# Eight gate modulation tiles of the second layer, computed among the first layer's heads instead of at the layer boundary

## The chip, the cores and the metric

The kernel runs on one core of a Trainium2 chip. The metric is the device time of one execution in microseconds (us); the kernel before was run three times. One execution was recorded by the hardware profiler, and its trace is what all rows below are read from. The engines are named as in the trace: PE is the matrix engine (PEld its weight loads), DVE the vector engine, ACT the scalar engine, POOL is GpSimd, SP issues transfers.

## The reference

One inference step of a two-layer decoder. T = 1088 token columns (1024 of a prompt, 8 x 8 of samples), D = 1024, 8 heads of 128. Each layer modulates a normalised input with shift and scale that come from a conditioning vector, mixes, projects out and adds the result with a gate from the same vector:

```python
def ada_modulate(x, c, norm_g, ada_w, ada_b):
    mod = jnp.einsum('bd,de->be', jax.nn.silu(c), ada_w) + ada_b
    shift, scale, gate = jnp.split(mod[:, None, :], 3, axis=-1)
    h = rms_norm(x, norm_g) * (1 + scale) + shift
    return h, gate

# layer 0, mixer_a: proj = h @ w_in; causal conv and silu on q, k, v; per head a gated
#   delta rule in chunks of 64 (a triangular solve per chunk, then a scan over the chunks);
#   o = rms_norm(o) * silu(z); y = o @ w_out
# layer 1, mixer_b: proj = h @ w_in; three groups of dilated window attention
#   (128, 1), (512, 4), (2048, 16), for samples over a cache of keys and values;
#   mixed by their log sums; y = (o * silu(z)) @ w_out
# x = x + gate * y after each layer; a last rms_norm
```

The `mod` row of one layer has 3072 columns, that is 24 tiles of 128: 8 of shift, 8 of scale, 8 of gate. A layer's gate is needed only when its output projection is added; its shift and scale are needed when its input is modulated.

## The kernel before, in words

All activations stand transposed: 128 features on the partitions, 1088 tokens along them, in three column chunks of 384, 384 and 320. `project` (L117 to L137) is one projection to 128 features: for each chunk, 8 k-tiles with three products each (hi by hi, hi by lo, lo by hi of operands split in two), 72 matmuls at L129, into one of two PSUM banks named pp; the third chunk takes the bank of the first once that has been copied out. Its weights come as one 512 KB transfer from SP's queue into `wraw` (L104, two buffers) and are split by ACT into `whi` (L110) and by DVE into `wlo` (L111), two buffers each.

One **modulation tile** (`ada_tile`, L145) is a 512 KB load of 128 columns of `ada_w`, 8 matmuls at L153 (the trace records each twice, so x16 is one tile), an ACT copy (`adr`, L155), one matmul at L160 (recorded twice too) and a DVE addition of the bias at L170, which writes `SH`, `SC` or `GT`. A generator (`ada_tiles`) hands out the tiles in a list, one for each credit that `ada.pump` gives.

Layer 0 runs over heads, in this program order: `stage_k(0)`, `stage_qv(0)`, `stage_k(1)`, `stage_inverse(0)`, and then for each head h: the scan of h, the q and v projections of h + 1, the k projection of h + 2 and the inverse of h + 1. So the projections come as k0, q0, v0, k1, q1, v1, k2 and so on; v0 is the v projection of head 0. Between them PE does small matmuls of the heads: kk products (L658), a short chain of powers for the inverse (`Us` and `su`, L680 to L693), transposes to natural order (L603), qk products (L740), the triangular inverse (L780 to L819), sample states (L845 to L913) and the scan (L932 to L946). The chain of the inverse needs the gates of all heads (`gall`, L522 to L526, and a round trip through memory, `gcscr` to `DT`, L646).

`conv_tile` (L549) is a projection of a head followed by the causal convolution; it ends with `ada.pump(1)`, except for k0. So 23 of the 24 listed tiles (layer 0's gate, layer 1's shift and scale) are handed out in the heads through `wraw`, and one more by `ada.pump(100)` after them (L1005).

At the layer boundary layer 1's input is modulated (`modulate`, L193 to L214): a column pass of 768 first, under the out projection, and then a last pass of 320 columns, tile by tile (j = 0 to 7). Each j takes some DVE operations (L72, the helper of scalar_tensor_tensor, and L201 to L210); ACT casts the result to `hh` and DVE or POOL subtracts to get `hl`. In this last loop (L1084 to L1086) each j is followed by `ada.pump(1)`, which hands out one of layer 1's eight gate tiles; their loads have a pool of their own, `aw`, of two buffers (`ada_load`, L139, transfer L142).

After it come layer 1's set-up (masks `mt` and `mdec` at L1133, three masks `Z` set to zero at L1140) and its first projection, of V in group 2 and head 0, whose result is copied out of PSUM at L1178 on DVE, 128x384 for the first two chunks. K's copies stand at L1176 on ACT.

A scheduler sets the order of the instructions on each engine from the program and its own estimates; an engine then works its list off in that order, each instruction waiting for what it needs. So an edit in one place can move instructions of many others.

Of the kernel before, what the change touches and what calls it, by code (L numbers as in the profile page):

```python
# [8 lines left out]
F32 = mybir.dt.float32  # L9
# [5 lines left out]
P = 128  # L15
D = 1024
KD = D // P
# [25 lines left out]
def kernel(ctx, tc, I, O):  # L43
# [58 lines left out]
    def wraw(src, n=P):  # L102
        t = wp.tile([P, KD, P], F32, name="wraw", bufs=2)
        SY.dma_start(out=t[:, :, :n], in_=src.rearrange("(k p) n -> p k n", p=P))  # L104
        return t
# [30 lines left out]
                        next(woven[0], None)  # L136
            cb(ci, acc)  # L137

    def ada_load(layer, ct, pool, ahead):  # L139
        src = I["ada_w"][layer, :, ct * P:(ct + 1) * P]  # L140
        t = pool.tile([P, KD, P], F32, name="aw", bufs=ahead)
        SY.dma_start(out=t, in_=src.rearrange("(k p) n -> p k n", p=P))  # L142
        return t

    def ada_tile(layer, ct, w):  # L145
        ada_fold(layer, ct, ada_rows(w))

# [92 lines left out]
            if not self.todo:  # L240
                self.credit = 0.0

    def ada_tiles(pool, todo):
        def load(i):
            layer, ct = todo[i]
            return ada_load(layer, ct, pool, 2) if pool else wraw(I["ada_w"][layer, :, ct * P:(ct + 1) * P])
        w = load(0) if pool else None
        for n, (layer, ct) in enumerate(todo):
            nxt = load(n + 1) if pool and n + 1 < len(todo) else None
            ada_tile(layer, ct, w if pool else load(n))  # L250
            w = nxt
            yield

    ada = Units()
    ada.todo.append(ada_tiles(None, [(0, c) for c in range(16, 24)] + [(1, i + o) for i in range(8) for o in (8, 0)]))


    W0 = I["a_w_in"][0]
# [45 lines left out]
    with tc.tile_pool(name="n0", bufs=1) as n0:  # L304
        aw = []
# [243 lines left out]
    def conv_tile(t, dst):  # L549
        w = wsplit(wraw(W0[:, t * P:(t + 1) * P]), G if 8 <= t < 16 else V)  # L550
        prev = [None]

        def cb(ci, acc):
            cn = CHUNKS[ci][1]
            xin = sb.tile([P, 387], F32, name="xin", bufs=2)
            if ci == 0:
                G.memset(xin[:, 0:3], 0.0)
            else:
                G.tensor_copy(out=xin[:, 0:3], in_=prev[0][:, 384:387])
            prev[0] = xin  # L560
            if ci < 2:
                A.copy(out=xin[:, 3:3 + cn], in_=acc[:, :cn])
                W = cn
            else:
                A.copy(out=xin[:, 3:259], in_=acc[:, :256])
                xs = xin[:, 259:347].rearrange("p (b x) -> p b x", x=11)
                G.tensor_copy(out=xs[:, :, 0:3], in_=scT[:, t, :].rearrange("p (b i) -> p b i", i=3))
                A.copy(out=xs[:, :, 3:11], in_=sview(acc[:, 256:320]))
                W = 344
                cst = sb.tile([P, 27], F32, name="cst", bufs=2)  # L570
                G.tensor_copy(out=cst[:, 0:3], in_=xin[:, 256:259])
                G.tensor_copy(out=cst[:, 3:27].rearrange("p (b i) -> p b i", i=3), in_=xs[:, :, 8:11])
                ct = acc[:27, 320:320 + P]
                PE.transpose(ct, cst, ident)
                cso = sb.tile([27, P], F32, name="cso", bufs=2)
                V.tensor_copy(out=cso, in_=ct)
                SY.dma_start(out=conv_p[:, t * P:(t + 1) * P], in_=cso[0:3, :])
                SY.dma_start(out=conv_s[:, t * P:(t + 1) * P], in_=cso[3:27, :])
            ca = sb.tile([P, 387], F32, name="ca", bufs=2)
            A.activation(out=ca[:, :W], in_=xin[:, 0:W], func=AF.Copy, scale=cwT[:, 0, t:t + 1])  # L580
            for i in range(1, 4):
                stt(ca[:, :W], xin[:, i:i + W], cwT[:, i, t:t + 1], ca[:, :W], ALU.mult, ALU.add)
            th = xin
            A.activation(out=th[:, :W], in_=ca[:, :W], func=AF.Tanh)
            c0 = CHUNKS[ci][0]
            if ci < 2:
                stt(dst[:, c0:c0 + cn], th[:, :cn], 1.0, ca[:, :cn], ALU.add, ALU.mult)
            else:
                stt(dst[:, c0:NP], th[:, :256], 1.0, ca[:, :256], ALU.add, ALU.mult)
                v1 = th[:, 259:347].rearrange("p (b x) -> p b x", x=11)[:, :, 0:8]  # L590
                v2 = ca[:, 259:347].rearrange("p (b x) -> p b x", x=11)[:, :, 0:8]
                stt(sview(dst[:, NP:]), v1, 1.0, v2, ALU.add, ALU.mult)
        project(w, hh, hl, cb)
        if t != 8:
            ada.pump(1)

    def banks_natural(src):
        out = []
# [409 lines left out]
    first.close()  # L1008
    set_banks(ctx, ps=3, lv=2, sc=1)

    aps = ExitStack()
    ap = aps.enter_context(tc.tile_pool(name="ap", bufs=1, reuse_waits="tile"))
    zp = ExitStack()
    zpool = zp.enter_context(tc.tile_pool(name="zp", bufs=1, reuse_waits="tile"))
    oh[7], ol[7] = (zpool.tile([P, T], F32R, name=n) for n in ("oh7", "ol7"))
# [47 lines left out]
    x1scr = [dr.tile([P, T], F32, name=f"x1scr{j}") for j in range(KD)]  # L1063
    x1 = [Columns("hh", F32) for _ in range(KD)]
    hh, hl = new_h()
    ada.todo.append(ada_tiles(ap, [(1, c) for c in range(16, 24)]))
    with tc.tile_pool(name="mid", bufs=1, reuse_waits="tile") as mp:
        def norm(qs, b0, b1):
            rn = col_stats(qs, b0, b1)
            rB = mp.tile([P, WIDE], F32, name="rB")  # L1070
            row_bcast(rB, rn, b0, b1)
            return rB

        def post(j):
            SY.dma_start(out=x1scr[j][:, :WIDE], in_=x1[j][:, :WIDE])

        def post2(j):
            SY.dma_start(out=x1scr[j][:, WIDE:], in_=x1[j][:, WIDE:])
            modulate(1, j, x1[j], rB, mp, hh, hl, 0, WIDE, True)
        qs = out_project(mp, 0, I["a_w_out"][0], xscr, x1, oh, ol, post, PASSES[0])  # L1080
        rB = norm(qs, 0, WIDE // P)
        qs = out_project(mp, 0, I["a_w_out"][0], xscr, x1, oh, ol, post2, PASSES[1])
        rB = norm(qs, WIDE // P, NC + 1)
        for j in range(KD):  # L1084
            modulate(1, j, x1[j], rB, mp, hh, hl, WIDE, T, j % 2 and j < KD - 1)
            ada.pump(1)  # L1086
    zp.close()
    aps.close()
    l0.close()


# [45 lines left out]
    Z = [sd.tile([P, ZW * n], F32, name=f"Z{g}").rearrange("p (b x) -> p b x", b=2 * NB)  # L1137
         for g, n in enumerate((1, 4, 8))]
    for t in Z:
        V.memset(t, 0.0)  # L1140
    odS = sd.tile([P, 512], F32, name="odS")
    G.memset(odS, 0.0)
    comb = sd.tile([P, 4, NL], F32, name="comb")
# [18 lines left out]
    def proj_tile(g, part, h, dst, dsts):  # L1162
        col = ((part * NG + g) * NH + h) * P
        w = wsplit(wraw(W1_[:, col:col + P]))

        def cb(ci, acc):
            c0, cn = CHUNKS[ci]
            n = cn if ci < 2 else cn - NS
            todo = [(perm(dst, g, c0, n), pin(acc, g, n))]
            if ci == 2:  # L1170
                todo.append((dsts[:, h % 2, :], acc[:, n:cn]))
            for o, i in todo:
                if part == 0:
                    A.activation(out=o, in_=i, func=AF.Copy, scale=-SCALE)
                elif part == 1:
                    A.copy(out=o, in_=i)  # L1176
                else:
                    V.tensor_copy(out=o, in_=i)  # L1178
        project(w, hh, hl, cb)

    def to_natural(src, nat, blocks, eng):
# [420 lines left out]
```

## Time and profile before

| | us |
|---|---|
| median of 3 runs | 2420.28 |
| lowest, highest | 2412.72, 2430.17 |
| the profiled execution's own time | 2412.29 |
| its span in the trace | 2410.6 |
| mean granted clock of PE | 0.962 of full speed |

The span runs from the first to the last instruction; 1.7 us of the execution lie around it. The profiled execution lies 8.0 us under the median, at the fast end of the runs. In a row, "x" counts instructions; a bracket in a timeline is the engine's idle time before the instruction and what ended it; the granted clock is a share of 2.4 GHz.

### The profile page before, as it was taken

How to read it: one execution, taken by the hardware profiler on the slowest of the kernel's cores; microseconds unless marked ns; L12 is line 12 of the kernel's file. 1: busy time of each engine (PE TensorE's matmuls, PEld its weight loads, DVE VectorE, ACT ScalarE, POOL GpSimd, SP SyncE). 2: the span in 40 equal slices, each digit the busy share in tenths (PEclk: the TensorE clock that was granted, in tenths of full speed). 3: DMA queues.
4: the chain of work that ended last, by engine and by line, in shares of the span. 5: the costliest groups of instructions: out<-in, count | busy, mean ns of one | idle time of the engine just before them, and what ended most of it. 6: DMA issues, size and time to landing. Idle time of an engine off the chain costs nothing.

```text
span 2410.6 us, 43253 instructions
## 1 busy us (share of the span) xinstructions
PE 2250.9 (93%) x16647; PEld 2116.5 (88%) x16647; DVE 1375.5 (57%) x3414; ACT 937.6 (39%) x2477; POOL 257.6 (11%) x418
## 2 busy tenths in 40 slices
PE   7899889999999998999998999899998999999998
PEld 5788778788888997999898999899998999989897
DVE  6678767867784437336733555434655336375334
ACT  5445445455443325233233332333323333234234
POOL 2213322333221103100000000000000000000000
PEclk9889989899999999999999999999999999999998
DMA  9223222223333445448822697535966349786634
GB/s 314 69 74 86 76 68 76 79 69 91 79 87 89 120 149 162 131 146 265 272 66 71 218 301 246 167 100 183 332 222 211 98 143 337 198 267 180 203 101 149
DMA packets 482255, 379.42 MB, mean 157 GB/s; under 512 B 46206, under 2 KB 457071, under 8 KB 482048
## 3 DMA queue, kind: packets, MB, share of 16 engines
q1 hardware_dynamic: 482048, 376.65, 51.6%
q8 instruction: 131, 2.15, 0.4%
q14 instruction: 76, 0.62, 0.1%
HBM read 322.31 MB, written 54.27 MB: 156 GB/s over the span
## 4 chain that ended last, share of the span: by engine, by line
PE 65%; DMA 11%; DVE 11%; issue 7%; ACT 3%; POOL 1%; SPq 1%; POOLq 0%; ACTq 0%; DVEq 0%
PE pp L129 47%; PE ps L1238 2%; PE ps L1220 2%; DMA DT<-gcscr 2%; PE sc L1438 2%; DMA wraw<-in_a_w_in_dram 2%; DVE vtmp L713 2%; DMA qb<-qscr 1%; PE ps L1184 1%; DVE pr L1389 1%; PE ps L1229 1%; DVE ca L72 1%; DMA oscr<-stgc 1%; PE ps L153 1%; DMA out_y_p_dram<-yn 1%
## 5 line engine op out<-in xcount | busy, mean ns | idle before, releaser
L129 PE MATMUL pp<-hh,whi 128*128 128x384 f32 (+1 forms) x2688 | 914.3, 341 | 14.5 <-DVE vT L1178 5.8
L129 PE MATMUL pp<-hl,whi 128*128 128x384 f32 (+1 forms) x2688 | 904.0, 336 | 1.3 <-POOL hl L214 1.3
L129 PE MATMUL pp<-hh,wlo 128*128 128x384 f32 (+1 forms) x2688 | 900.8, 335 | 2.0 <-DVE wlo L111 2.0
L129 PEld LDWEIGHTS pp<-hh,whi 128*128 128x128 f32 x2688 | 512.5, 191 | 29.8 <-DVE vT L1178 8.5
L129 PEld LDWEIGHTS pp<-hl,whi 128*128 128x128 f32 x2688 | 512.8, 191 | 6.6 <-issue 1.9
L129 PEld LDWEIGHTS pp<-hh,wlo 128*128 128x128 f32 x2688 | 511.3, 190 | 7.7 <-issue 2.9
L111 DVE TENSOR_TENSOR wlo<-wraw,whi 128x1024 fp32r<-128x1024 f32 x136 | 171.2, 1259 | 131.3 <-ACT whi L110 130.5
L110 ACT CAST whi<-wraw 128x1024 fp32r<-128x1024 f32 x144 | 150.7, 1046 | 230.0 <-PE pp L129 148.2
L1225 ACT ACTIVATE sm<-sm,stg 128x128 f32<-128x128 f32 (+1 forms) x192 | 86.6, 451 | 340.4 <-DVE stg L1223 299.8
L1389 DVE TENSOR_TENSOR pr<-kc,qb 128x1024 f32<-128x1024 f32 x128 | 154.9, 1218 | 85.2 <-DMA qb<-qscr 55.7
L1379 DVE TENSOR_REDUCE ST<-pr 128x8 f32<-128x1024 f32 x128 | 153.7, 1213 | 1.1
L438 POOL TENSOR_TENSOR ol<-zo,oh 128x384 fp32r<-128x384 f32 x9 | 9.1, 1013 | 1311.4 <-ACT oh L437 1291.2
L72 DVE SCALAR_TENSOR_TENSOR ca<-xin,cwT,ca 128x384 f32<-128x384 f32 (+1 forms) x216 | 129.0, 601 | 7.1 <-ACT ca L580 5.9
L1223 DVE CUSTOM_DVE_ANT_0 sm<-ps,mA 128x256 f32<-128x256 f32 (+1 forms) x128 | 48.3, 377 | 139.4 <-PE ps L1220 138.2
L1238 PE MATMUL ps<-vnat,pT 128*128 128x128 f32 x560 | 97.1, 281 | 8.1 <-DVE pT L1234 6.4
L713 DVE TENSOR_TENSOR vtmp<-Vi,Mi 128x2 f32<-128x2 f32 (+30 forms) x248 | 99.0, 399 | 4.2 <-POOL so L88 0.7
L1238 PEld LDWEIGHTS ps<-vnat,pT 128*128 128x128 f32 x560 | 86.1, 190 | 14.3 <-issue 4.8
L1220 PE MATMUL ps<-kT,qT 128*128 128x128 f32 (+1 forms) x384 | 93.5, 325 | 1.2 <-DVE stg L1223 1.2
L1232 ACT COPY pT<-ps 128x256 f32<-128x256 f32 (+1 forms) x96 | 32.4, 337 | 119.3 <-PE ps L1229 118.4
L72 DVE SCALAR_TENSOR_TENSOR hh<-pp,GT,xr 128x384 f32<-128x384 f32 (+1 forms) x48 | 27.4, 571 | 82.4 <-PE pp L129 78.7
L129 PE MATMUL pp<-oh,whi 128*128 128x384 f32 (+1 forms) x216 | 71.7, 333 | 2.7 <-DVE zt L72 2.7
L129 PE MATMUL pp<-oh,wlo 128*128 128x384 f32 (+1 forms) x216 | 71.9, 334 | 1.5 <-DVE wlo L111 1.5
(449 smaller groups left out, 3556.1 us busy)
## 6 DMA issues: line engine op xcount, KB each, us to landing
qb<-qscr SPq DMA_DIRECT2D x128, 512.0 KB
kc<-in_cache_kv_w_dram SPq DMA_DIRECT2D x104, 512.0 KB
vc<-in_cache_kv_w_dram SPq DMA_DIRECT2D x104, 512.0 KB
wraw<-in_b_w_in_dram SPq DMA_DIRECT2D x80, 512.0 KB
wraw<-in_a_w_in_dram SPq DMA_DIRECT2D x32, 512.0 KB
wraw<-in_ada_w_dram SPq DMA_DIRECT2D x24, 512.0 KB
stgc<-gscr SPq DMA_DIRECT2D x32, 260.0 KB
aw<-in_ada_w_dram SPq DMA_DIRECT2D x8, 1024.0 KB
```

Of the source, the lines that this page charges most:

```text
L72: return (eng or V).scalar_tensor_tensor(out=out, in0=in0, scalar=scalar, in1=in1, op0=op0, op1=op1)
L110: A.copy(out=hi, in_=raw)
L111: (eng or V).tensor_tensor(out=lo, in0=raw, in1=hi.bitcast(F32), op=ALU.subtract)
L129: mm = PE.matmul(acc[:, :cn], lhsT=a[:, k, :], rhs=b[k][:, c0:c0 + cn], start=(n == 0), stop=(n == 3 * KD - 1))
L713: V.tensor_tensor(out=tv, in0=Vi[:, :na, :w], in1=Mi[:, :w, c].unsqueeze(1).broadcast_to([P, na, w]), op=ALU.mult)
L1220: PE.matmul(sv, lhsT=qT[:, b * P:(b + 1) * P], rhs=kT[:, k0:k0 + w], start=True, stop=True)
L1223: V.tensor_tensor_reduce(out=sm[:, :w], in0=sv, in1=mk, scale=1.0, scalar=3e38, op0=ALU.add, op1=ALU.min, accum_out=stg[:, b, 128:129])
L1225: A.activation(out=sm[:, :w], in_=sm[:, :w], func=AF.Exp, scale=-1.0, bias=stg[:, b, 128:129], accum_out=stg[:, b, 129:130])
L1238: PE.matmul(ob[:, (b % 4) * P:(b % 4 + 1) * P], lhsT=pT[:, i * P:(i + 1) * P], rhs=vnat[:, k0 // P + i, :], start=(i == 0), stop=(i == w / ...
L1379: V.tensor_reduce(out=sv[:, n:n + 4, :], in_=pr.rearrange("p (n a e) -> p n a e", a=2, e=P), op=ALU.add, axis=AX.X)
L1389: V.tensor_tensor(out=out, in0=k, in1=q, op=ALU.mult)
L1438: mm = PE.matmul(od[32 * j:32 * j + 8, f * P:(f + 1) * P], lhsT=Z[g][:, a * NB + 2 * j + c, 8 * k:8 * k + 8], rhs=vc[:, j, a * P:(a + 1) * P],
```

## The change

It does three things. The eight gate tiles of layer 1 go into the same list as the other 24 and are loaded through `wraw`; `ada_load` and the pool `aw` go. The pump in `conv_tile` gives three credits instead of one after q0, v0 and k1 (t = 0, 16 and 9), so that the 23 pumps hand out 29 of 32 tiles and `ada.pump(100)` the last three. The three masks `Z` are set to zero by POOL instead of DVE. The first V projection, and that alone, is copied out of PSUM by ACT instead of DVE.

```diff
-    def ada_load(layer, ct, pool, ahead):
-        src = I["ada_w"][layer, :, ct * P:(ct + 1) * P]
-        t = pool.tile([P, KD, P], F32, name="aw", bufs=ahead)
-        SY.dma_start(out=t, in_=src.rearrange("(k p) n -> p k n", p=P))
-        return t
...
-    def ada_tiles(pool, todo):
-        def load(i):
-            layer, ct = todo[i]
-            return ada_load(layer, ct, pool, 2) if pool else wraw(I["ada_w"][layer, :, ct * P:(ct + 1) * P])
-        w = load(0) if pool else None
-        for n, (layer, ct) in enumerate(todo):
-            nxt = load(n + 1) if pool and n + 1 < len(todo) else None
-            ada_tile(layer, ct, w if pool else load(n))
-            w = nxt
+    def ada_tiles(todo):
+        for layer, ct in todo:
+            ada_tile(layer, ct, wraw(I["ada_w"][layer, :, ct * P:(ct + 1) * P]))
             yield
...
-    ada.todo.append(ada_tiles(None, [(0, c) for c in range(16, 24)] + [(1, i + o) for i in range(8) for o in (8, 0)]))
+    ada.todo.append(ada_tiles([(0, c) for c in range(16, 24)] + [(1, i + o) for i in range(8) for o in (8, 0)]
+                              + [(1, c) for c in range(16, 24)]))
...
-            ada.pump(1)
+            ada.pump(3 if t in (0, 16, 9) else 1)
...
-    ada.todo.append(ada_tiles(ap, [(1, c) for c in range(16, 24)]))
...
             modulate(1, j, x1[j], rB, mp, hh, hl, WIDE, T, j % 2 and j < KD - 1)
-            ada.pump(1)
...
     for t in Z:
-        V.memset(t, 0.0)
+        G.memset(t, 0.0)
...
-                    V.tensor_copy(out=o, in_=i)
+                    (A.copy if (g, h) == (2, 0) else V.tensor_copy)(out=o, in_=i)
```

The order of the instructions moves at three places that matter here. Numbers at a row's start are places in an engine's list; in the changed kernel the lines after the first edit are six to eleven lower (the modulation matmul L153 is L147 there, the fold L160 is L154, the transposes L603 are L592, the kk products L658 are L647).

**PE, head 0, after q0's last matmul (row 216).** Before, v0 follows at once, and the clump of small matmuls comes after v0:

```order
217 L522 MATMUL ps<-gall,tri 128x64
222 L129 MATMUL pp<-hh_417,whi 128x384
...
298 L129 MATMUL pp<-hh_761,wlo 128x320
299 L658 MATMUL ps<-kT_854 128x128 x4
303 L680 MATMUL ps<-ident,Us 64x64
307 L153 MATMUL ps<-wraw,cT 32x128 x8
310 L693 MATMUL ps<-su 64x64
311 L603 MATMUL ps<-ident,qT_1265 128x128 x8
312 L129 MATMUL pp<-hh_417,whi 128x384
```

Now the clump comes first, with the three tiles of q0's pump in it, and row 240 is v0's first matmul:

```order
221 L129 MATMUL pp<-hh_761,wlo 128x320
223 L592 MATMUL ps<-ident,kT_854 128x128 x8
226 L647 MATMUL ps<-kT_854 128x128 x8
229 L669 MATMUL ps<-ident,Us 64x64
233 L147 MATMUL ps<-wraw,cT 32x128 x8
236 L682 MATMUL ps<-su 64x64
237 L147 MATMUL ps<-wraw,cT 32x128 x16
239 L592 MATMUL ps<-ident,qT_1265 128x128 x8
240 L129 MATMUL pp<-hh_417,whi 128x384
...
315 L147 MATMUL ps<-wraw,cT 32x128 x16
318 L147 MATMUL ps<-wraw,cT 32x128 x8
322 L129 MATMUL pp<-hh_417,whi 128x384
```

So the clump has moved ahead of v0, and rows 315 and 318 are v0's three tiles, ahead of k1 at row 322; k1's three follow in the same way ahead of q1. On SP the loads of weights in this stretch read so before (rows 16 and 17 are the first tile's and v0's, 41 is k1's, 45 is q1's):

```order
16 L104 DMA wraw<-in_ada_w_dram 128x8x128
17 L104 DMA wraw<-in_a_w_in_dram 128x8x128
...
28 L104 DMA wraw<-in_ada_w_dram 128x8x128
...
41 L104 DMA wraw<-in_a_w_in_dram 128x8x128
42 L104 DMA wraw<-in_ada_w_dram 128x8x128
43 L104 DMA wraw<-in_a_w_in_dram 128x8x128
```

and now so, where row 38 is v0's load, row 40 k1's and row 48 q1's:

```order
16 L104 DMA wraw<-in_ada_w_dram 128x8x128 x2
...
37 L104 DMA wraw<-in_ada_w_dram 128x8x128
38 L104 DMA wraw<-in_a_w_in_dram 128x8x128
39 L104 DMA wraw<-in_ada_w_dram 128x8x128 x3
40 L104 DMA wraw<-in_a_w_in_dram 128x8x128
43 L104 DMA wraw<-in_ada_w_dram 128x8x128
45 L104 DMA wraw<-in_ada_w_dram 128x8x128
47 L104 DMA wraw<-in_ada_w_dram 128x8x128
48 L104 DMA wraw<-in_a_w_in_dram 128x8x128
```

The two `wraw` buffers hold the first two tiles from the start, so that v0's load has moved behind the matmuls of the second tile.

**PE, head 1's inverse and head 2's chain, in the ninth projection.** Before, these follow each other with no matmul of a projection between them:

```order
788 L790 MATMUL lv<-VT,MT_1873 32x32 x11
...
798 L798 MATMUL lv<-Vt_2042,Aw 32x32 x16
801 L806 MATMUL lv<-ident,Vt_2042 64x64 x8
806 L813 MATMUL lv<-VT,MT_1873 64x64 x8
812 L819 MATMUL lv<-Vt_2042,Aw 64x64 x8
817 L845 MATMUL lv<-Vt_2042,kn 128x128
828 L886 MATMUL lv<-Sb,kqz_834 32x128 x16
837 L913 MATMUL lv<-wm,kds 128x512
841 L574 MATMUL pp<-ident,cst 27x128
```

Now the inverse comes after the chain and between matmuls of projections (L769 and L779 are L780 and L790 of before), and the sample states later still:

```order
823 L147 MATMUL ps<-wraw,cT 32x128 x8
829 L592 MATMUL ps<-ident,qT_3483 128x128 x4
...
854 L769 MATMUL lv<-ident,Vt_2133 128x128 x7
...
876 L779 MATMUL lv<-VT,MT_1964 32x32 x4
...
889 L787 MATMUL lv<-Vt_2133,Aw 32x32 x16
890 L729 MATMUL ps<-qT_3483,kT_2854 128x128 x8
```

The clump of before has been taken apart; from head 2's chain on each projection has one modulation tile in both kernels, at like places.

**PE, the layer boundary.** Before, tiles stand between the first two chunks of the first V projection and its third:

```order
3756 L222 MATMUL ps<-ident,rn 128x64
3757 L153 MATMUL ps<-aw,cT 32x128 x16
3758 L160 MATMUL ps<-fold,adr 128x9
3759 L129 MATMUL pp<-hl_11235,whi 128x384
...
3764 L153 MATMUL ps<-aw,cT 32x128 x14
3770 L153 MATMUL ps<-aw,cT 32x128 x16
3772 L153 MATMUL ps<-aw,cT 32x128 x8
3773 L160 MATMUL ps<-fold,adr 128x9
3774 L129 MATMUL pp<-hh_11256,whi 128x320
```

Now nothing stands there:

```order
3789 L216 MATMUL ps<-ident,rn 128x64
3790 L129 MATMUL pp<-hl_11352,whi 128x384
3791 L129 MATMUL pp<-hh_11351,wlo 128x384
3792 L129 MATMUL pp<-hl_11352,whi 128x384
3793 L129 MATMUL pp<-hh_11351,wlo 128x384
3794 L129 MATMUL pp<-hh_11373,whi 128x320
```

On ACT the two copies of V's first chunks stand behind the last cast to `hh`, and on POOL the three masks stand behind the last `hl` (L214) and ahead of `mt`.

## Rows read from the trace of the kernel before

**Rows 1.** The page's busy times and instructions, by engine.

```profile
PE 2250.9 (93%) x16647; PEld 2116.5 (88%) x16647; DVE 1375.5 (57%) x3414; ACT 937.6 (39%) x2477; POOL 257.6 (11%) x418
```

**Rows 2.** Windows: length, then PE, PEld, DVE, ACT, POOL busy, granted clock, DMA.

```profile
101.40:123.30 21.90, 9.46 (x53) 6.67 (x52) 16.41 (x65) 8.35 (x25) 4.34 (x10) 0.57 0.41 99
240.00:266.00 26.00, 21.11 (x182) 16.47 (x181) 18.93 (x63) 13.70 (x45) 9.37 (x14) 0.85 0.28 79
...
951.00:972.00 21.00, 12.80 (x152) 9.36 (x152) 13.95 (x53) 8.06 (x25) 5.46 (x14) 0.66 0.70 205
```

**Rows 3.** Chain, head 0: start, length, work.

```profile
93.66 8.72 DMA DT<-gcscr
...
105.20 0.47 DVE vT L72
...
114.19 0.49 DVE ca L72
...
117.02 1.01 PE ps L153 x16
118.09 4.05 DMA wraw<-in_a_w_in_dram
```

**Rows 4.** PE's waits, 101 to 123.5 us: total, times, longest.

```profile
PE ps L658 <- ACT kN L635: 3.5, 1, 3.5
```

**Rows 5.** PE's timeline, head 0: start, length, line, out<-in, count.

```profile
123.26 0.69 PE L129 MATMUL pp<-hh,whi 128*128 128x384 f32 x1 [1.95 <-ACT whi L110]
...
144.13 0.34 PE L129 MATMUL pp<-hh,whi 128*128 128x384 f32 x1
...
146.49 0.64 PE L153 MATMUL ps<-wraw,cT 128*32 128x128 f32 x16
...
158.21 0.34 PE L129 MATMUL pp<-hh,whi 128*128 128x384 f32 x1
...
164.31 1.03 PE L780 MATMUL lv<-ident,Vt 128*128 128x128 f32 x8
...
184.01 1.14 PE L819 MATMUL lv<-Vt,Aw 64*64 64x64 f32 x16
```

**Rows 6.** PE's waits, 240 to 264 us.

```profile
PE lv L845 <- ACT kn L841: 1.6, 1, 1.6
```

**Rows 7.** Chain, layer boundary.

```profile
952.55 5.85 DMA aw<-in_ada_w_dram
...
971.78 4.89 PE pp L129 x23
```

**Rows 8.** DVE's timeline, layer boundary; idle before and releaser in brackets.

```profile
960.17 0.23 DVE L170 TENSOR_SCALAR GT<-ps,vecs 128x9 f32<-128x9 f32 x1 [2.15 <-PE ps L160]
...
961.70 0.23 DVE L170 TENSOR_SCALAR GT<-ps,vecs 128x9 f32<-128x9 f32 x1 [0.64 <-PE ps L160]
...
968.47 0.23 DVE L170 TENSOR_SCALAR GT<-ps,vecs 128x9 f32<-128x9 f32 x1 [0.98 <-PE ps L160]
...
969.15 0.22 DVE L170 TENSOR_SCALAR GT<-ps,vecs 128x9 f32<-128x9 f32 x1
969.28 0.21 DVE L210 TENSOR_TENSOR hl<-tmp,hh 128x64 fp32r<-128x64 f32 x1
969.41 1.48 DVE L1178 COPY vT<-pp 128x384 f32<-128x384 f32 x2
...
972.89 0.91 DVE L1140 MEMSET Z<- 128x1024 f32 x1 [0.16 <-issue]
```

**Rows 9.** PE's timeline, layer boundary.

```profile
971.63 0.61 PE L129 MATMUL pp<-hh,whi 128*128 128x320 f32 x1
```

**Rows 10.** SP's timeline, layer boundary.

```profile
952.11 13.93 SPq L142 DMA_DIRECT2D aw<-in_ada_w_dram  x6
```

**Rows 11.** Lines 719 and 1176: duration ns min/median/max, first and last start, forms.

```profile
L719 POOL MEMSET Vt<- x8: 951/951/959, 69.4 to 596.6; 128x1024 f32 x8
...
L1176 ACT COPY kT<-pp x72: 357/624/888, 981.4 to 2125.5; 128x384 f32<-128x384 f32 x48, 128x256 f32<-128x256 f32 x24
```

More of the change, by code (lines that the diff above doesn't have):

```diff
@@ L1009 @@
     set_banks(ctx, ps=3, lv=2, sc=1)
-    aps = ExitStack()
-    ap = aps.enter_context(tc.tile_pool(name="ap", bufs=1, reuse_waits="tile"))
     zp = ExitStack()
@@ L1085 @@
             modulate(1, j, x1[j], rB, mp, hh, hl, WIDE, T, j % 2 and j < KD - 1)
-            ada.pump(1)
     zp.close()
-    aps.close()
     l0.close()
```

## The prediction, made before the changed kernel was run

> **What bounds the kernel now.** I read the busy times first, then windows of PE, then the waits and the chain inside the windows that stand out. PE is busy for 93% of the span [rows 1], so the kernel is a row of matmuls, and a change can move the time only by adding or removing PE work or by opening or closing gaps on PE. The reader is to see three such gaps [rows 2]. At the layer boundary PE works 12.80 of 21.00 us at a granted clock of 0.66 of full speed, that is partly at 1.2 GHz. In head 0 it works 9.46 of 21.90 us, at 0.57. In head 1 it works 21.11 of 26.00 us, at 0.85. The change touches all three.
>
> At the boundary the chain goes through the load of a modulation tile, which takes 5.85 us in a burst of such loads [rows 7]. DVE stands three times behind a fold that is waiting for its tile, and does the last `hl` at 969.28 and V's copies right after [rows 8]; PE starts V's third chunk at 971.63 [rows 9]. In head 0 the chain waits 8.72 us for the gates' round trip, then goes through DVE, among them eight pieces of v0's convolution of about half a microsecond each, the first at 105.20 and the last at 114.19, and then through a tile and the next weights' load [rows 3]; PE's longest wait is for `kN` [rows 4].
>
> **The change, term by term.**
>
> The boundary. The eight tiles leave it. DVE loses the three fold waits, 2.15 + 0.64 + 0.98 = 3.8 us, and seven folds ahead of the last `hl`, which by the starts at 969.15 and 969.28 cost 0.13 each, 0.9 [rows 8]. So the last `hl` comes 4.7 earlier. V's first bank was free at 969.41 + 1.48 / 2 = 970.15, yet PE started at 971.63, because its list had tiles ahead; these 1.5 go too. ACT's copy takes up to 0.89 against 0.74 on DVE [rows 11, 8], +0.15. Together -6.0. Low end: only the first two waits come back (2.8), since the modulation then waits for its own casts. High end: V's third chunk, 4.9 us long [rows 7], runs under the casts, -11. I take -6.0, the sum that the rows give for one fixed order of DVE.
>
> The masks and the SP queue. POOL writes 128x1024 zeros in 0.95, DVE in 0.91 [rows 11, 8]; they come after the last `hl` of POOL, and nothing before layer 1's first sample attention reads them, so 0 (without that cover 1.5 us, by 0.95 for 1024 columns and in proportion for the 512 and 128 of the others). SP's six issues of tiles took 13.93 of its queue [rows 10]; what stands behind them can now be issued earlier, and no PE wait in this stretch names it: 0.
>
> The tail of the heads. Three tiles instead of one are left for the last pump. A tile warm is 0.64 on PE [rows 5] plus its fold, which I count as 0.16: 0.8, so two cost +1.6 (0 if they fall in a gap, 3 if their loads are late).
>
> Head 0. This is the large term. v0's matmuls, which covered the gates' round trip, now stand behind the clump, and v0's load stands behind the second tile's matmuls. In the kernel before, the load after the clump's tile was issued at 118.09, landed 4.05 later, and its first matmul came at 123.26, 1.1 after that [rows 3, 5]. In the new order the clump's DVE chain is free of v0's convolution, -4.0; but the rest of the chain (1.1) and a second tile (1.0) come ahead of the issue. So v0's load is issued at 118.1 - 4.0 + 2.1 = 116.2 and v0 starts at 121.4. k1 took 20.9 at this place (123.26 to 144.13) and q1 14.1 (144.13 to 158.21) [rows 5]; v0 has the cold clock of the one and fewer waits, so I take the middle, 17.5: it ends at 138.9. Then two tiles (1.3), k1's load (4.05) and split (1.1): k1 starts at 145.4, ends 14.1 later at 159.5, and by the same 6.5 q1 starts at 166.0. It started at 144.13, so it is 21.9 late. By then the inverse of head 0 is done, which before came after: six groups between the two rows of lines 780 and 819 [rows 5], about 5.7 us. That leaves +16.2 us lost at q1's start, six tiles among it. Low end: both late loads are covered by other PE work (-8.1, so +8). High end: v0 takes k1's 20.9 (+19.6).
>
> Head 1. Its inverse and the sample states no longer stand in one clump. The idle time there, 26.00 - 21.11 = 4.9, goes, its longest wait for `kn` among it [rows 2, 6], and the clock need not fall: 0.15 of 21.1 busy us is 3.2. Together -8.1 (0 if it comes back in another place).
>
> From head 2's chain on, each projection has one tile in both kernels, so I count nothing there.
>
> The bursts. After q0, v0 and k1 two or three tiles are loaded beside the next weights. One load alone took 4.05 [rows 3], one in a burst 5.85 [rows 7]; I take 4.05, because PE frees the buffers one after the other and so spaces the loads out. By the other row each of three loads is 1.8 later, +5.4. The Trainium skill, page "DMA: Bandwidth & Descriptors", section "Issuing engines are not separate DMA queues", says that transfers run on the same 16 DMA engines and interleave, whoever issued them, which speaks for the longer row. With the figure of that page's section on bandwidth, 1 MB in 6.15 us, a pair of these loads would land in 6.15, an estimate of +2.1 for each of the three and +6.3 for the sum.
>
> Sum: -6.0 + 1.6 + 16.2 - 8.1 = +3.7. Against the profiled execution, 2412.3, that is 2416.0; this execution lies 8.0 under the median of the runs, so against the median 2424.0. About 1% (24 us) is what a measurement of this kernel can tell from no change, so this is no change.
>
> **The rivals.**
>
> *Late weights in every head (slower).* One weight load per head comes to stand behind a tile, as v0's and k1's do: 4.05 in each of seven later heads, 28.4, so 2424.0 + 28.4 = 2452.4. It decides once a head loses more than 2.9 us (3.7 + 7 x 2.9 = 24). For it: 29 of 32 tiles share two buffers with all weights. Against: after head 2's chain the orders have the tiles at like places. Chance 0.08.
>
> *The chain gets ahead (lower).* The inverse of head 0 is done a projection earlier; if the lead lasts, one more clump of head 1's kind, 8.1, goes, and the boundary gives its high end, another 5.0: 2424.0 - 13.1 = 2410.9. For it: the second clump really is taken apart in the order. Against: head 1's inverse itself stands later than before. 0.20.
>
> *Nothing comes back.* Head 1 keeps its idle time in other places and the boundary gives 2.8: -2.8 + 1.6 + 16.2 = +15.0, so 2435.3. For it: PE's waits in these clumps are for DVE and ACT, whose work the change leaves. 0.15.
>
> *The bursts land late.* +5.4 on the sum, so 2429.4. For it: the row of 5.85 and the rule beside it. Against: the spacing. 0.12.
>
> **The numbers.** My forecast, with 0.45, is 2424. Its own range, with the small ends, is 2416 to 2433. The range that should hold the time 8 times in 10 takes in the third and fourth rival and most of the second: 2406 to 2442. Faster than 2396 needs the second rival and more, 0.04. Slower than 2444.5 is the first rival and the upper edge of the third, 0.10. The rest, 0.86, is within 1%.
>
> **What would show it.** In the changed profile: no L147 matmul and no fold wait on DVE at the boundary, and V's third chunk about 1 us after the last cast; v0 at about 121, k1 at 145, q1 at 166, each started by ACT's `whi` behind a load; a gap on PE ahead of v0 with only the clump in it; no stretch like 240 to 266 with the clock under 0.9. If q1 starts near 150, head 0 was costed too dear and the time falls with it; if the later heads show waits for `whi`, the first rival holds. A lost lead would show as new waits for `kn` or `Us` between 170 and 330.

## The result, and the profile after

The changed kernel takes 2440.56 us (median of 8 runs, 2436.41 to 2454.27), the kernel before 2418.35 (8 runs, 2409.58 to 2431.87). The ratio is 1.0098, 95% interval [1.0077, 1.0119]: slower by about 22 us, where 3.7 were forecast. The two traces are 28.5 us apart (spans of 2439.1 and 2410.6), because the profiled execution of before lies low among its runs; so sizes read from that pair run some 6 us high.

The busy times of the page, after (before: [rows 1]):

```profile
PE 2273.2 (93%) x16647; PEld 2136.5 (88%) x16647; DVE 1372.8 (56%) x3407; ACT 944.7 (39%) x2481; POOL 255.3 (10%) x421
```

PE does the same 16647 instructions in 22.3 us more of busy time. Only 6 of the 28.5 us are more idle time; the rest is the same work done more slowly, at a mean granted clock of 0.952 instead of 0.962. The clock of whole runs says the same: 0.946 to 0.955 in the eight of the change, 0.952 to 0.966 in the 88 of the kernel before that were timed beside the experiments.

Where it went shows best in stretches cut at the first matmuls of certain projections: k0 to q1, q1 to the seventh z projection (the z projections follow the heads), and, as the boundary, layer 1's first projection to its second. Windows of before, with length, busy time of each engine and granted clock:

```profile
35.87:144.13 108.26, 92.56 (x692) 78.83 (x692) 79.53 (x246) 49.47 (x139) 29.75 (x45) 0.86 0.42 127
144.13:804.61 660.48, 616.29 (x4824) 544.19 (x4822) 490.51 (x1480) 320.32 (x1030) 173.25 (x295) 0.96 0.31 81
...
935.86:976.77 40.91, 28.59 (x231) 23.95 (x230) 25.46 (x69) 16.68 (x37) 16.48 (x23) 0.75 0.61 185
```

and the same stretches after:

```profile
35.90:174.87 138.97, 112.61 (x940) 94.89 (x939) 96.00 (x287) 57.77 (x164) 30.73 (x51) 0.82 0.44 128
174.87:839.51 664.64, 630.92 (x4720) 557.41 (x4719) 476.26 (x1447) 317.81 (x1015) 168.83 (x288) 0.92 0.31 81
...
971.42:1006.37 34.95, 19.25 (x86) 17.37 (x85) 21.49 (x56) 16.55 (x30) 18.05 (x26) 0.71 0.40 120
```

The first stretch is 30.7 us longer: 20.0 of them are busy time, mostly of the six more tiles and of head 0's inverse, which before came later, and 10.7 are idle. The second stretch is 4.2 longer, the boundary 6.0 shorter; the rest is together 0.4 shorter. In the second, PE's idle time (length less busy) fell from 44.2 to 33.7, and yet the stretch grew: PE was busy 14.6 us longer with 104 fewer recorded matmuls, at 0.92 of full speed instead of 0.96.

PE's timeline after, at the first matmuls of v0, k1 and q1:

```profile
122.38 0.69 PE L129 MATMUL pp<-hh,whi 128*128 128x384 f32 x1
...
145.69 0.69 PE L129 MATMUL pp<-hh,whi 128*128 128x384 f32 x1
...
174.87 0.67 PE L129 MATMUL pp<-hh,whi 128*128 128x384 f32 x1
```

and the chain between them (start, length, work):

```profile
113.63 1.01 PE ps L147 x16
114.64 0.06 PE ps L680
114.70 3.54 DMA wraw<-in_ada_w_dram
118.25 0.14 issue
118.38 1.11 PE ps L147 x16
...
137.72 0.62 PE ps L147 x16
138.34 0.02 issue
138.36 3.95 DMA wraw<-in_ada_w_dram
142.30 0.14 issue
142.44 1.08 PE ps L147 x16
```

This is the pattern of a triple pump. The third tile's load can be issued only when the first tile has left its buffer, and on PE the first tile's matmuls stand behind the projection's last one: they start at 137.7 in this chain, the third tile's matmuls only at 142.44, and k1 at 145.69. Before q1 tiles, the rest of the inverse and transposes fill the gap, at a mean granted clock of 0.72.

At the layer boundary, PE, then ACT, then DVE, after:

```profile
1001.04 0.63 PE L129 MATMUL pp<-hh,whi 128*128 128x320 f32 x1 [12.53 <-ACT vT L1162]
```

```profile
1000.02 0.24 ACT L203 CAST hh<-tmp 128x64 fp32r<-128x64 f32 x1
1000.17 1.48 ACT L1162 COPY vT<-pp 128x384 f32<-128x384 f32 x2
```

```profile
1000.45 0.22 DVE L204 TENSOR_TENSOR hl<-tmp,hh 128x64 fp32r<-128x64 f32 x1
```

V's third chunk starts 0.87 after its first bank's copy begins, and that right behind the last cast; no fold is left on DVE (before: [rows 8, 9]). ACT takes 1.48 for the two copies, as DVE did [rows 8].

### The profile page after: what moved, and what is told of

It reads as the page before. It is cut to its first block, busy times and chain, and to the rows that moved or that the text cites. A ratio compares the mean times of both kernels' runs of the same rounds, so it can differ in the third digit from the quotient of the medians.

```text
span 2439.1 us, 43228 instructions
## 1 busy us (share of the span) xinstructions
PE 2273.2 (93%) x16647; PEld 2136.5 (88%) x16647; DVE 1372.8 (56%) x3407; ACT 944.7 (39%) x2481; POOL 255.3 (10%) x421
## 4 chain that ended last, share of the span: by engine, by line
PE 72%; DMA 11%; DVE 10%; ACT 3%; issue 2%; SPq 1%; POOL 1%; POOLq 0%; ACTq 0%; DVEq 0%
PE pp L129 51%; PE ps L1204 2%; PE ps L1222 2%; DMA DT<-gcscr 2%; PE sc L1422 2%; DVE pr L1373 1%; PE ps L1168 1%; DMA qb<-qscr 1%; DMA kc<-in_cache_kv_w_dram 1%; PE ps L1213 1%; DMA oscr<-stgc 1%; PE ps L147 1%; DVE vtmp L702 1%; DMA stgc<-gscr 1%; PE ps L592 1%
## 5 line engine op out<-in xcount | busy, mean ns | idle before, releaser
L702 DVE TENSOR_TENSOR vtmp<-Vi,Mi 128x2 f32<-128x2 f32 (+30 forms) x248 | 91.5, 369 | 4.0 <-PE ps L682 0.7
L1207 DVE CUSTOM_DVE_ANT_0 sm<-ps,mG 128x128 f32<-128x128 f32 x64 | 18.4, 288 | 97.1 <-PE ps L1204 67.7
```

What stands on the lines that cost most here:

```text
L702: V.tensor_tensor(out=tv, in0=Vi[:, :na, :w], in1=Mi[:, :w, c].unsqueeze(1).broadcast_to([P, na, w]), op=ALU.mult)
L1207: V.tensor_tensor_reduce(out=sm[:, :w], in0=sv, in1=mk, scale=1.0, scalar=3e38, op0=ALU.add, op1=ALU.min, accum_out=stg[:, b, 128:129])
```

## The experiments

All edits are against the changed kernel unless said otherwise; ratios are against the kernel before, timed on the same chip. In the order of the pumps, t = 0 is q0, 16 v0, 9 k1, 1 q1.

**heads_only**, the three larger pumps alone, put into the kernel before:

```diff
-            ada.pump(1)
+            ada.pump(3 if t in (0, 16, 9) else 1)
```

> The kernel before, with three credits instead of one after q0, v0 and k1; layer 1's gate tiles stay at the boundary, masks and V copy as before. Theory A (the loss lies in the heads, in the order that the three larger pumps bring about): the boundary stays at its old length, so this is slower than the changed kernel by the 6.0 us of the boundary and faster by the two extra tiles of the tail (1.6): about 34 us over before, 1.4%. Theory B (the loss comes from 8 more tiles going through the two weight buffers, wherever they stand): the same 24 tiles as before go through them, so about 0.

2438.13, ratio 1.0082 [1.0058, 1.0107]. The loss is in the heads, and 24 tiles are enough for it: theory B falls. A's 34 was too high: it was counted from the low trace of before. From the medians A gives 22.2 + 6.0 - 1.6 = 26.6, just above the measured interval of 14 to 26. The windows are near those of the change in the first two stretches, and the boundary is no shorter than before:

```profile
35.19:171.19 136.00, 110.75 (x939) 93.73 (x939) 96.58 (x287) 58.22 (x164) 31.11 (x51) 0.83 0.46 132
171.19:830.02 658.83, 629.25 (x4576) 557.62 (x4575) 474.99 (x1439) 316.83 (x1007) 172.34 (x288) 0.91 0.29 75
961.31:1004.41 43.10, 30.98 (x231) 25.45 (x230) 25.56 (x70) 17.04 (x37) 16.66 (x23) 0.68 0.58 178
```

**setup_only**, the masks and the V copy alone, in the kernel before:

```diff
-        V.memset(t, 0.0)
+        G.memset(t, 0.0)
...
-                    V.tensor_copy(out=o, in_=i)
+                    (A.copy if (g, h) == (2, 0) else V.tensor_copy)(out=o, in_=i)
```

> The kernel before with the masks zeroed by POOL and the first V tile copied by ACT, no tile moved. Both theories: within 2 us of before, since PE's list at the boundary still has the tiles ahead of V's third chunk. A third theory (these two edits cost something in layer 1, by POOL or ACT): slower by 3 us or more.

2420.72, ratio 1.0005 [0.9983, 1.0028]: these two edits alone cost nothing and bring nothing.

**tail** and **outproj** leave the heads with one credit each (the first edit), and put the eight gate tiles behind them, among the z projections (tail) or one after each out projection of the first pass (outproj, which has the second edit too):

```diff
-            ada.pump(3 if t in (0, 16, 9) else 1)
+            ada.pump(1)
```

```diff
-                              + [(1, c) for c in range(16, 24)]))
...
     ada.pump(100)
+    ada.todo.append(ada_tiles([(1, c) for c in range(16, 24)]))
...
             SY.dma_start(out=x1scr[j][:, :WIDE], in_=x1[j][:, :WIDE])
+            ada.pump(1)
```

> The changed kernel with one credit everywhere, so that nine tiles are left for the pump after the heads; its heads have the order of before. Theory A: the boundary's 6.0 us come back and eight tiles of 0.8 us go between the z projections, where PE has few gaps: 0 against before, from -3 to +3. Theory B: eight more tiles through the two weight buffers cost a load each, 8 x 4 = 32 less 6, so +26.

> The changed kernel with one credit in the heads and layer 1's gate tiles handed out one after each of the eight out projections of the first pass; the order gathers them between the last z projection and the out projection. Theory A: the boundary's 6.0 come back, 8 x 0.8 = 6.4 of PE work are added where no chain waits, and the loads of the tiles stand in a row of two buffers there (8 x 4 / 2 = 16 us, of which the gap before the out projection covers some): from 0 to +10 against before. Theory B: +26 as for the tail.

tail: 2424.89, ratio 1.0029 [1.0006, 1.0052]; no row is read from its trace. outproj: 2416.39, ratio 0.9987 [0.9962, 1.0012]. Eight more tiles through the two weight buffers do not cost 26 us, so B falls again. By the ratios the tail stands at +7 (+1 to +13) against A's -3 to +3, and outproj at -3 (-9 to +3) against 0 to +10: both lie outside A's ranges, but both intervals reach into them.

**q0only, v0only, k1only**: three credits after one of the three projections alone, and **q0one**: the triple moved from q0 to q1.

```diff
-            ada.pump(3 if t in (0, 16, 9) else 1)
+            ada.pump(3 if t == 0 else 1)         # q0only; 16: v0only; 9: k1only; in (16, 9, 1): q0one
```

> The changed kernel with three credits after q0 alone and one elsewhere; six tiles are left for the pump after the heads, as against eight extra in the run named tail (2424.9). Theory A1 (the loss comes from the pump after q0, which puts v0 behind the clump of head 0): most of the heads' loss stays, +15 to +25 against before. Theory A2 (each of the three pumps costs about the same, a late weight load each): +7 on the tail's time, so about +11 against before.

> The same with three credits after v0 alone; v0 keeps its old place ahead of the clump, and three tiles stand between the clump and k1. Theory A1: little, from 0 to +8 against before. Theory A2: about +11.

> The same with three credits after k1 alone; heads as before up to k1, then three tiles ahead of q1. Theory A1: little, from 0 to +8. Theory A2: about +11.

> The changed kernel with the triple credit moved from q0 to q1: three credits after v0, k1 and q1, three tiles left at the end as in the change. v0 keeps its old place. Theory A1: the loss of the pump after q0 is gone, so within 6 of before. Theory A2: three late loads as in the change, so +20.

q0only: 2418.62, ratio 1.0008 [0.9985, 1.0031]. v0only: 2428.28, 1.0047 [1.0023, 1.0070]. k1only: 2407.4, 0.9961 [0.9940, 0.9982]. q0one: 2412.87, 0.9979 [0.9954, 1.0004]. Neither theory holds for the whole time: A1 falls by q0only, where v0 stands behind the clump as in the change and nothing is lost in the end; A2 fits v0only (+11) but falls by the other three. In the first stretch alone, though, A2 has the right form. A table from the windows of each trace, in us against before, with the granted clock of the second stretch:

| run | k0 to q1 | q1 to seventh z | clock there |
|---|---|---|---|
| before | 108.3 | 660.5 | 0.96 |
| setup_only | -1.0 | +1.4 | 0.95 |
| outproj | -1.7 | +6.3 | 0.94 |
| q0only | +9.0 | -1.0 | 0.94 |
| v0only | +8.5 | +10.3 | 0.94 |
| k1only | +7.2 | -12.3 | 0.94 |
| q0one | +14.3 | -15.3 | 0.94 |
| the change | +30.7 | +4.2 | 0.92 |
| heads_only | +27.7 | -1.7 | 0.91 |
| inside | +20.7 | -8.8 | 0.95 |
| two | +23.8 | -0.6 | 0.94 |
| k1out | +7.3 | -23.8 | 0.96 |
| skip3 | +29.4 | -4.3 | 0.93 |
| skip19 | +28.9 | +4.4 | 0.92 |

In setup_only and outproj PE has before's order up to the seventh z projection. Their rows show how far executions of one order lie apart: 1.7 us up to q1, 6.3 behind it, at a clock of 0.94 to 0.96.

Up to q1 the three single pumps nearly add up: 9.0 + 8.5 + 7.2 = 24.7, against 27.7 to 30.7 for all three in four traces; v0's and k1's give 15.7, against 14.3 in q0one. After q1 no such sum holds. In q0only PE's timeline also shows the clean opposite of the pattern above, k1 following v0's single tile at once:

```profile
137.92 0.65 PE L147 MATMUL ps<-wraw,cT 128*32 128x128 f32 x16
138.49 0.55 PE L592 MATMUL ps<-ident,vT 128*128 128x128 f32 x3
138.80 0.43 PE L129 MATMUL pp<-hh,whi 128*128 128x384 f32 x1
```

v0 starts there at about the same time as in the change, so k1's 6.9 us (145.69 against 138.80) are the two extra tiles.

**inside** gives the same three credits to the same projections, one after each column chunk. **two** gives two. **late** keeps head 0 at one and gives two after eight projections of heads 4 to 7. **k1out** joins k1only with outproj for the six tiles that are left.

```diff
+            if t in (0, 16, 9):                  # inside, at the end of the callback of a chunk
+                ada.pump(1)
...
-        if t != 8:
+        if t not in (8, 0, 16, 9):              # inside
...
-            ada.pump(3 if t in (0, 16, 9) else 1)
+            ada.pump(1)                                                 # inside
+            ada.pump(2 if t in (0, 16, 9) else 1)                       # two
+            ada.pump(2 if t in (4, 5, 6, 7, 20, 21, 22, 23) else 1)     # late
+            ada.pump(3 if t == 9 else 1)                                # k1out
```

> The changed kernel with the same three credits for q0, v0 and k1, but given one after each column chunk, inside the projection, instead of three after it, so that some of the tiles' matmuls come between the projection's and free their weight buffers earlier. Theory C (a second and a third tile after a projection keep both weight buffers until the projection is over, so the next weights are loaded only then, about 8 us of gap before k1 and before q1): k1 and q1 start earlier by most of this, and the time is from 0 to +8 against before. Theory D (the number of tiles in head 0 and the clock that falls there cost, wherever in a projection they stand): about +20 as the change.

> The changed kernel with two credits instead of three after q0, v0 and k1; five tiles are left for the pump after the heads. Theory C: one late load less at each of the three places, about 4 us each, and 3 for the two more tiles in the tail: +10 to +14 against before. Theory D (cost by the number of tiles, three instead of six more in head 0): about +10 as well; it tells C from a threshold at three: with a threshold, about +3.

> The changed kernel with one credit in head 0 and two credits after each of eight later projections (q and v of heads 4 to 7), so that head 0 keeps the order of before. Theory C: a late load of some 5 us at each of eight places, part of it beside the chain's waits, less the boundary's 6: from +10 to +34. Theory E (only head 0 has no other work to put into the gap, later heads have the scan): from -6 to +6.

> Three credits after k1 alone, and the six tiles that are left one after each out projection of the first pass instead of among the last z projections. By the runs named k1only (2407.4) and outproj (2416.4, against 2424.9 for the tail): 8.5 less than k1only, less 2 because it is six tiles and not eight, so about 2401, -18 against before. A theory in which the runs differ only by chance of the order gives no such sum: anything from -15 to +10.

inside: 2419.21, ratio 0.9994 [0.9974, 1.0015]. The same tiles, given inside the same projections, cost nothing in the end, so D falls and C's forecast of the time holds. In its trace a weights' load stands on the chain where the change has a tile's:

```profile
141.83 4.03 DMA wraw<-in_a_w_in_dram
```

Of the change's loss up to q1, only 10 of 30.7 us are gone, and 13 more go after q1, which C does not explain.

two: 2437.98, ratio 1.0064 [1.0038, 1.0090], or +15 (9 to 22). The threshold at three falls; C and D are not told apart, since the interval holds both forecasts. Two tiles cost most of what three cost up to q1, +23.8, which is 6.9 less where C counted 12. Two tiles already fill both weight buffers; that this is the reason was not tested.

late: 2424.64, ratio 1.0020 [0.9993, 1.0047], or +5 (-2 to +11). That is in theory E's range, but the interval reaches C's lower end, and E's reason, that later heads have other work for such gaps, is not borne out. PE's waits for weights after q1 (total, times, longest) are these, 15.8 us together, against 4.2 in before:

```profile
PE pp L129 <- ACT whi L110: 9.5, 5, 2.5
PE pp L129 <- DVE wlo L111: 6.3, 2, 5.8
```

k1out: 2400.41 (4 runs), ratio 0.9909 [0.9876, 0.9942], where the forecast from the two runs that it joins was 2401. It is faster than both kernels.

**skip3** and **skip19** leave heads 0 and 1 as in the change and take one credit away, after q3 or v3, so that PE's order differs only from the eleventh projection on.

```diff
-            ada.pump(3 if t in (0, 16, 9) else 1)
+            ada.pump(3 if t in (0, 16, 9) else 0 if t == 3 else 1)      # skip3; 19: skip19
```

> The changed kernel with no credit after q3 (t = 3), so that one tile more is left for the pump after the heads. PE's order is the changed kernel's up to the eleventh projection; after that the clump of head 4 (small matmuls with none of a projection between them, in the eighteenth projection) has 42 rows instead of 47 and that of head 3, which the change had split, is back with 47. Theory F (what is lost after head 1 comes from the length of these runs of small matmuls, clump by clump): the stretch of projections 15 to 18 takes about 80 us instead of 93, that of 12 to 15 about 87 instead of 83, and the time is about 10 below the change, 2431. Theory G (what head 0 lost is simply carried on, whatever the later order): 15 to 18 as in the change, 92, and 2440.

> The same with no credit after v3 (t = 19) instead. Head 4's clump keeps 47 rows but holds less in matrix work (9.7 against 11.0 us at full clock by the rows' shapes), and head 3's is back with 42. Theory F: between the change and the run named skip3, about 2435; 15 to 18 about 86. Theory G: 2440 and 92.

skip3: 2436.71, ratio 1.0075 [1.0052, 1.0099]. skip19: 2436.46, 1.0081 [1.0058, 1.0105]. The windows from k5's first matmul to k6's (the forecast's projections 15 to 18, counted from 0), of before, the change, skip3 and skip19:

```profile
450.75:527.25 76.50, 71.02 (x595) 65.09 (x595) 57.88 (x187) 40.05 (x131) 22.51 (x41) 0.98 0.32 83
```

```profile
472.44:565.69 93.25, 84.45 (x607) 74.50 (x607) 71.51 (x227) 44.33 (x146) 23.08 (x46) 0.84 0.27 68
```

```profile
474.44:560.21 85.77, 79.18 (x606) 68.84 (x605) 66.86 (x207) 43.29 (x146) 26.81 (x43) 0.92 0.27 70
```

```profile
474.60:556.25 81.65, 77.43 (x597) 70.71 (x598) 61.78 (x205) 42.66 (x142) 23.59 (x46) 0.90 0.29 73
```

In this stretch F is right in direction: another order gives back 7 to 12 us of it, mostly as busy time at a higher clock. But F gave the larger gain to skip3 (80, and 86 for skip19), and 7.5 us is little more than one order varies: before's order took 80.7 and 80.5 here in setup_only and outproj. The change's own order took 91.9 in heads_only. From k4 to k5 skip3 took 87.2 and the change 83.3, as F said. On the whole time neither theory is decided: skip3 lies between F's 2431 and G's 2440, skip19 near F's 2435, and both intervals overlap that of the change. What is lost up to q1 stays in both (+29.4 and +28.9).

## Why the prediction was wrong

**The boundary** was right: -6.0 forecast, 40.91 - 34.95 = 6.0 measured, and by the step that was given. V's third chunk follows the copy, the copy the last cast. Only ACT's +0.15 was not there.

**v0 and k1** started where they were forecast, at 122.38 and 145.69 for 121.4 and 145.4, and the load of each stood behind tiles as the order said. That k1 came so near is in part luck: v0 took 15.3 us where 17.5 were counted (137.72 - 122.38), and the gap behind it 8.0 where 6.5 were counted.

**q1** was 8.9 late on the forecast, 174.87 against 166.0. Two windows of the change show why, k1 and the gap behind it:

```profile
145.69:163.84 18.15, 17.32 (x118) 15.88 (x116) 9.95 (x20) 4.55 (x10) 3.45 (x5) 0.84 0.25 60
163.84:174.87 11.03, 10.05 (x137) 8.68 (x136) 6.22 (x15) 6.13 (x18) 0.72 (x5) 0.72 0.52 145
```

k1 took 18.15 us where 14.1 were counted, since its clock was 0.84 and the first groups of head 0's inverse stood among its matmuls. The step "by the same 6.5" was mis-sized too, at 11.03. I let the inverse run beside the weights' load for nothing; in the list the rest of it stands between k1's end and q1, with the three tiles, and PE worked it off at 0.72 of full speed. The second and third tile of a pump, which hold both weight buffers until the projection is over, I had as 6.5 per projection; a single pump costs 7.2 to 9.0 up to q1.

**Head 1 and after** is where the forecast failed, by two steps. One is head 1: -8.1, "the idle time there ... goes ... and the clock need not fall", which with the inverse done early (-5.7) gave -13.8 from q1 to k4. The other is "from head 2's chain on ... I count nothing there", which with the tail gave +1.6 from k4 to the seventh z projection. These two stretches, of before and then of the change:

```profile
144.13:364.04 219.91, 202.50 (x1626) 176.97 (x1625) 172.60 (x524) 110.06 (x358) 60.12 (x109) 0.94 0.30 77
364.04:804.61 440.57, 413.79 (x3201) 367.23 (x3199) 317.91 (x957) 210.25 (x674) 113.13 (x187) 0.97 0.32 83
```

```profile
174.87:389.13 214.26, 202.26 (x1487) 176.93 (x1485) 164.01 (x516) 105.09 (x340) 58.02 (x102) 0.92 0.31 81
389.13:839.51 450.38, 428.66 (x3237) 380.48 (x3235) 312.25 (x932) 212.72 (x677) 110.81 (x186) 0.92 0.31 81
```

The first came out at -5.7 instead of -13.8, and in heads_only, with the same order there, at -1.4. Its idle time did go, 5.4 us of it where I counted 4.9; but 139 recorded matmuls fewer kept PE busy for the same 202 us, at 0.92 instead of 0.94. I had read a full PE as a fast PE. The second came out at +9.8 instead of +1.6, and at +8.3 and +2.4 against setup_only and outproj (442.1 and 448.0). Its clear loss is k5 to k6 above, 93.25 against 76.5 to 80.7: the tiles stand at like places there, the other small matmuls do not. Later heads gave part of it back.

Over both stretches a mean of 0.92 is 16% of the time at half speed and 0.96 is 8%, by which some 50 us more were at 1.2 GHz than in the trace of before; against outproj's 0.94 it is about half of that, by the same estimate. The four traces with the change's head 0 have 0.91 to 0.93, the three with before's order 0.94 to 0.96. heads_only is among the four with the tiles of the boundary left in place, so by these few traces the clock goes with the order of the heads; by which rows of that order it falls was not settled.

**The sum.** Against the forecast of +3.7, the missing 24.8 us of the trace are 8.8 before q1 and 16.4 after it (8.2 in each of the two stretches), less 0.4 elsewhere. Some 6 of the 24.8 are the low trace of before.

**The rivals.** Late weights in every head did not come: after q1 PE waited 1.3 us for `whi`, 2.9 before. The chain did not get ahead; what came was the loss of head 0, most of it kept. "Nothing comes back", at 2435.3, was the nearest, and by luck: its mechanism, PE held by DVE and ACT in the clumps, is not what the windows show, since PE's idle time shrank. So it is also luck that the time lies inside the range up to 2442, which was drawn to take in that rival. Bursts did not matter: the tiles' loads on the chain took 3.54 and 3.95 us, as a single one had (4.05 [rows 3]). The Trainium skill's rule on shared DMA engines, page "DMA: Bandwidth & Descriptors", section "Issuing engines are not separate DMA queues", therefore made no difference here; the buffers spaced the loads out.

**What stays open.** Up to q1 the costs nearly add up. After q1 the orders made by different pumps in head 0 end between 24 us faster and 10 slower than before, while one order varies by 6, and only from k5 to k6 was it shown that the order there matters. That it is the held buffers that cost the time up to q1 rests on q0only and inside, which gave back 6.9 us before k1 and 10 before q1; the rest of the 30.7, part of which is work that stood later before, was not split further. Why k1only's and k1out's order gains so much, and q0one's, was not settled. That forcing an old later order behind the new head 0 would restore the time was not tried, and neither was a third weight buffer.

## What to carry to other kernels

Work moved into "idle" places through buffers that it shares with the main stream must free them before the main stream asks again: the same 3 x 3 tiles cost 22 us when handed out after a projection and nothing when handed out inside it, though only about 10 us of that could be seen where the tiles stand. Where a scheduler sets the order, forecast the place that you can read from its list, and put a wide range on everything after it; moving one pump changed heads that it does not touch by more than it cost itself. And when idle time goes but small matmuls take its place, look at the granted clock before counting the gain.

## What the runs showed of the hardware

A PE that shows as full can still be at the low clock. In the change, head 4's run of small matmuls, with none of a projection between them, lasts from 515.05 to 529.60. PE shows no idle time in it, and the clock is at 2.4 GHz at first and at 1.2 GHz from 520.20 on:

```profile
515.05:520.20 5.15, 5.15 (x90) 4.39 (x89) 2.15 (x8) 3.12 (x10) 1.17 (x3) 1.00 0.31 78
520.20:529.60 9.40, 9.40 (x75) 7.68 (x74) 2.61 (x13) 3.90 (x11) 0.85 (x2) 0.50 0.33 93
```

The ends of matmuls are modelled in the trace, so short gaps between them may not show.

The Trainium skill, page "TensorE: Matmul & The Clock Gate", section "HAM oscillation — how this bites in real kernels", tells of the same loss of clock where PE waits for data and has nothing to do; these rows show it without such a wait.

And the clock differs between executions of one order. k1only and k1out have the same list on PE up to the end of the heads, yet the stretch from k4 to k5 took 80.06 us in the one's trace and 73.96 in the other's:

```profile
369.94:450.00 80.06, 76.06 (x595) 69.13 (x593) 57.17 (x187) 40.75 (x134) 24.79 (x41) 0.90 0.29 75
```

```profile
364.43:438.39 73.96, 69.84 (x594) 63.48 (x593) 57.17 (x185) 39.67 (x131) 24.87 (x40) 1.00 0.31 82
```

So a difference of 6 us between two single traces, in a stretch full of small matmuls, says nothing by itself; the medians and the repeated orders do.
